# A bidirectional hybrid layer on one Trainium2 core: gate row, decays, weight rounding, key loads and z gates at other places of the order

## The chip, the core and the metric

The kernel runs on one core of one Trainium2 chip. The metric is the device time of one execution in microseconds (us). The kernel before took 1383.26 us, the median of three runs (1382.79 to 1388.96).

TensorE multiplies matrices into result tiles in PSUM, VectorE and ScalarE work on them, GpSimd does what is left of elementwise work, and SyncE issues most DMA transfers. ScalarE and GpSimd issue some as well. Each engine takes its instructions in its own order.

## The reference, cut to what matters

One layer on 2048 tokens of 1024 numbers, all in float32:

```
shift, scale, gate = split(silu(c) @ w_ada + b_ada)
h    = rmsnorm(x, norm_w) * (1 + scale) + shift
proj = h @ w_in + b_in    # na_q na_k na_v na_z (512 each), ml_q ml_k ml_v ml_o ml_z (512 each), 4 gate rows of 4
na   = neighbourhood_attention(na_q, na_k, na_v, rpb) * silu(na_z)     # 8 heads, windows of 8 x 16
q, k = split(silu(short_conv(concat(ml_q, ml_k))))
hm   = (mlstm(q, k, ml_v, gates) + flip(mlstm(flipped ...))) * sigmoid(ml_o)   # 4 heads
ml   = headnorm(hm) * ml_norm_w * silu(ml_z)
x    = x + gate * (concat(na, ml) @ w_out);  out = rmsnorm(x, final_norm_w)
```

The mLSTM runs in chunks. Inside a chunk the scores q k are multiplied by exp(Dlog - m), a triangular matrix of decays for each direction.

## The kernel before

**Matmuls.** Each float32 operand is split into a rounded part (hi) and a rest (lo), and each product is three matmuls. ScalarE rounds the weights (whi, L195), GpSimd subtracts (wlo, L196), both from the tile raw that `load_w` loads on SyncE (L193).

**Stages.** `start` normalises the tokens, multiplies them by the modulation of c and makes the first products. `tok_blocks` (L557) then goes through four blocks of 256 columns, 16 tiles of 128 tokens each, in groups of four: blocks 2 and 3 by `vo_group` (values and output gates of the mLSTM, pvo, evicted to stvo by VectorE, L499) and blocks 4 and 5 by `nav_group` (values of the attention, pv, evicted to stv, L464). Blocks 0 and 1 go by the same `vo_group` inside `start`. There are four result tiles (pp) and two stage tiles that take turns. The store of a group (d_ck L506, d_vna L468) is put off to the end of the next one. `conv_blocks` (L752) makes queries and keys of the mLSTM: pc is evicted to u by ScalarE (L773), VectorE convolves (acc_k, L808), ScalarE applies silu (L809), TensorE transposes keys (kt, L819). `phase1b` goes through four heads; in each, `ml_pass1` makes the states from tiles kv (L1013) and `ml_pass2` the outputs from tiles ck (L1058). The rest of the projections, pq (L866), fills the gaps. `phase2` is the attention and the output projection.

**The side chain.** Beside the matmuls of `tok_blocks` a chain of small jobs advances one step per token tile (`next(self.chain, None)`):
- `gate_chain` (L577) turns the gate columns into decay columns, guards and the row matrix d_mneg;
- `decays` (L685) has 16 groups. Each loads one 128x1024 tile dec (both directions) with two loads of 256 KB from d_mneg on SyncE (L702), adds the triangular mask on GpSimd (L710), raises it with eight exponentials on ScalarE (L714) and stores it to d_ck with two stores from ScalarE's queue. Two tiles take turns;
- `gate_row` (L391) makes the gate of the residual: silu(c) times the last 1024 columns of w_ada, summed by VectorE (gsum, L408 and L410) over eight loads of 512 KB into the two halves of the tile wide (L401). It advances beside the decays, one step of it per group.

The places in the order follow from the program: SyncE's loads and stores stand where the code issues them. A load whose tile is still in use holds up everything behind it.

**The passes of the mLSTM.** `close_step` (L990) runs once per chunk step. It starts a pending key load (kk, L981, 512 KB, eight in all, back from d_kna into the tiles hhi and hlo that are free by then) every second step, once they are free. `normalise` (L1131) loads the z gates of a group of four chunks (`load_z`, zt, L1070) on ScalarE's queue into a single tile; the tile is stored to d_mix from ScalarE's queue too (L1155).

## Time and profile before

| what | value |
|---|---|
| median of three runs | 1383.26 us |
| the profiled execution | 1385.16 us, span 1383.4 us |
| mean granted clock of TensorE | 0.989 |
| busy: TensorE, VectorE, ScalarE, GpSimd | 1291.3, 792.3, 531.8, 284.1 us |
| moved by DMA | 263.29 MB, mean 190 GB/s |
| blocks 2 to 5 (`tok_blocks`) | about 160 to 360 us |
| `conv_blocks` | about 360 to 554 us |
| the heads of the mLSTM | about 554 to 1010 us |

A row of a timeline gives the start, the duration, the engine, the line and the instruction with what it writes and reads, and in square brackets how long the engine had been idle before it and what ended that. PE is TensorE, DVE VectorE, ACT ScalarE, POOL GpSimd, SP SyncE; a q behind the name marks what the engine's queue issues, such as DMA transfers. A row of waits gives the waiting engine and line, the engine and line waited for, and the total, the number and the longest.

### The profile page before, as it was taken

How to read it: one execution, taken by the hardware profiler on the slowest of the kernel's cores; microseconds unless marked ns; L12 is line 12 of the kernel's file. 1: busy time of each engine (PE TensorE's matmuls, PEld its weight loads, DVE VectorE, ACT ScalarE, POOL GpSimd, SP SyncE). 2: the span in 40 equal slices, each digit the busy share in tenths (PEclk: the TensorE clock that was granted, in tenths of full speed). 3: DMA queues.
4: the chain of work that ended last, by engine and by line, in shares of the span. 5: the costliest groups of instructions: out<-in, count | busy, mean ns of one | idle time of the engine just before them, and what ended most of it. 6: DMA issues, size and time to landing. Idle time of an engine off the chain costs nothing.

```text
span 1383.4 us, 23357 instructions
## 1 busy us (share of the span) xinstructions
PE 1291.3 (93%) x8204; PEld 1104.9 (80%) x8204; DVE 792.3 (57%) x2428; ACT 531.8 (38%) x1123; POOL 284.1 (21%) x306
## 2 busy tenths in 40 slices
PE   2989998998999999999989999899998999999996
PEld 2889998998887778788878878778876777778775
DVE  6683324111355569246767866767736666667664
ACT  4642334423232233213313322323346555555552
POOL 4343212424101011001212101212201211112121
PEclk9999999999999999999999999999999999999998
DMA  9799449787557685554675788555588996867871
GB/s 321 223 290 228 122 97 238 175 204 189 149 110 210 151 191 160 164 157 144 184 219 182 229 237 284 165 159 159 176 249 251 209 228 171 187 184 183 205 182 47
DMA packets 243272, 263.29 MB, mean 190 GB/s; under 512 B 31814, under 2 KB 200006, under 8 KB 243154
## 3 DMA queue, kind: packets, MB, share of 16 engines
q1 hardware_dynamic: 151774, 186.18, 49.8%
q0 software_dynamic: 20496, 36.21, 10.8%
q10 hardware_dynamic: 70884, 39.40, 9.9%
q8 instruction: 65, 1.06, 0.3%
q14 instruction: 53, 0.43, 0.1%
HBM read 177.18 MB, written 92.72 MB: 195 GB/s over the span
## 4 chain that ended last, share of the span: by engine, by line
PE 46%; DMA 11%; issue 4%; DVE 4%; POOL 1%; ACT 1%; ACTq 0%; SPq 0%; DVEq 0%; POOLq 0%
PE pq L866 19%; PE y L1429 9%; DMA tab<-d_t 4%; PE pT L1369 3%; PE pO L1384 2%; PE pS L1341 2%; PE pi L1090 2%; DMA kv<-d_ck 2%; PE px L1088 2%; PE pc L429 2%; PE pc L430 2%; PE pc L431 2%; DMA d_mix<-zt 2%; PE dc L1036 1%; DMA d_qna<-qst 1%
## 5 line engine op out<-in xcount | busy, mean ns | idle before, releaser
L866 PE MATMUL pq<-hhi,whi_a 128*128 128x512 f32 x512 | 208.6, 407 | 1.2 <-ACT u L773 0.8
L866 PE MATMUL pq<-hlo,whi_a 128*128 128x512 f32 x512 | 208.9, 408 | 0.0
L866 PE MATMUL pq<-hhi,wlo_a 128*128 128x512 f32 x512 | 208.2, 407 | 0.0
L866 PEld LDWEIGHTS pq<-hhi,whi_a 128*128 128x128 f32 x512 | 97.3, 190 | 18.9 <-ACT u L773 1.2
L866 PEld LDWEIGHTS pq<-hlo,whi_a 128*128 128x128 f32 x512 | 97.2, 190 | 16.8 <-issue 0.5
L866 PEld LDWEIGHTS pq<-hhi,wlo_a 128*128 128x128 f32 x512 | 97.3, 190 | 16.6
L1371 ACT ACTIVATE pt<-pT 96x384 f32<-96x384 f32 (+3 forms) x128 | 65.8, 514 | 84.5 <-PE pT L1369 81.3
L1350 ACT ACTIVATE pbuf<-pbuf,mn 128x480 f32<-128x480 f32 (+5 forms) x128 | 76.1, 595 | 54.1 <-DVE mn L1349 53.8
L1429 PE MATMUL y<-hhi,whi_a 128*128 128x512 f32 x256 | 90.6, 415 | 0.5 <-ACT whi_a L1399 0.5
L1429 PE MATMUL y<-hhi,wlo_a 128*128 128x512 f32 (+1 forms) x272 | 90.6, 399 | 0.2 <-ACT y L1436 0.2
L1349 DVE CUSTOM_DVE_ANT_0 pbuf<-pS,tab 128x480 f32<-128x480 f32 (+5 forms) x128 | 63.3, 540 | 40.3 <-PE pS L1341 29.6
L840 POOL TENSOR_TENSOR wlo_a<-rawq,whi_a 128x1024 fp32r<-128x1024 f32 x20 | 48.6, 2430 | 169.8 <-ACT whi_a L839 144.9
L1112 POOL TENSOR_TENSOR hm<-hm,ck 128x128 f32<-128x128 f32 x64 | 26.4, 413 | 260.3 <-DVE hm L1111 183.4
L429 PE MATMUL pvo<-whi_b,hhi 128*128 128x256 f32 x256 | 74.1, 289 | 5.7 <-DVE stvo L499 5.7
L1093 ACT ACTIVATE num<-px,gtile 128x129 f32<-128x129 f32 x120 | 38.3, 366 | 105.7 <-PE px L1088 88.0
L1020 DVE TENSOR_SCALAR wv<-kv,gtile 128x129 f32<-128x129 f32 x120 | 38.4, 329 | 67.1 <-DMA kv<-d_ck 33.5
L1369 PE MATMUL pT<-ident,pbuf 128*128 128x128 f32 (+2 forms) x416 | 66.8, 273 | 10.0 <-DVE pbuf L1361 8.5
L1369 PEld LDWEIGHTS pT<-ident,pbuf 128*128 128x128 f32 (+2 forms) x416 | 50.3, 136 | 31.9 <-issue 11.6
L430 PE MATMUL pvo<-wlo_b,hhi 128*128 128x256 f32 x256 | 72.8, 285 | 0.0
L431 PE MATMUL pvo<-whi_b,hlo 128*128 128x256 f32 x256 | 72.8, 284 | 0.0
L714 ACT ACTIVATE dec<-dec,gtile 128x128 f32<-128x128 f32 x128 | 42.0, 392 | 71.4 <-POOL dec L710 68.3
L499 DVE TENSOR_TENSOR stvo<-pvo,brow 128x256 f32<-128x256 f32 x64 | 26.5, 419 | 68.6 <-PE pvo L431 56.4
(295 smaller groups left out, 3432.6 us busy)
## 6 DMA issues: line engine op xcount, KB each, us to landing
ck<-d_ck SPq DMA_DIRECT2D x64, 384.5 KB
kv<-d_ck SPq DMA_DIRECT2D x120, 128.5 KB
rawq<-in_w_main_dram SPq DMA_DIRECT2D x28, 512.0 KB
raw<-in_w_main_dram SPq DMA_DIRECT2D x20, 512.0 KB
d_ck<-stvo SPq DMA_DIRECT2D x16, 514.0 KB
x<-in_x_dram SPq DMA_DIRECT2D x16, 512.0 KB
wada<-in_w_ada_dram SPq DMA_DIRECT2D x32, 256.0 KB
dec<-d_mneg SPq DMA_DIRECT2D x32, 256.0 KB
```

The lines of the kernel that those rows point to most:

```text
L429: nc.tensor.matmul(ps, lhi(k), rhi(k), start=(k == 0), stop=False)
L430: nc.tensor.matmul(ps, lhi(k), rlo(k), start=False, stop=False)
L431: nc.tensor.matmul(ps, llo(k), rhi(k), start=False, stop=(k == KT - 1))
L714: nc.scalar.activation(t[:, d, o, :], t[:, d, o, :], AF.Exp, bias=self.cols["g"][:, d, h, c : c + 1])
L840: nc.gpsimd.tensor_tensor(lo[:, :, cs], raw, hi[:, :, cs].bitcast(F32), ALU.subtract)
L866: nc.tensor.matmul(patch_ps(ps) if patch else ps, w, self.htok(h, g, k, patch), start=(k == 0 and n == 0), stop=(k == KT - 1 and n == 2))
L1020: nc.vector.tensor_scalar(wv, tiles[d, i][:, 128:257], self.cols["w"][:, d, h, c : c + 1], None, ALU.mult)
L1349: nc.vector.tensor_tensor_reduce(pt[:, :nk], ps, tabs[place[u]][j][:, :nk], 1.0, 3e38, ALU.add, ALU.min, mn)
L1350: nc.scalar.activation(pt[:, :nk], pt[:, :nk], AF.Exp, bias=mn, scale=-1.0, accum_out=sums[:, j : j + 1])
L1369: nc.tensor.transpose(ps[:cs, i, :], U[u][j][:, i * cs : (i + 1) * cs], self.ident)
L1371: nc.scalar.activation(t[:cs, :nch, :], ps[:cs, :nch, :], AF.Copy)
L1429: nc.tensor.matmul(y, m[:, k, :], w[k][:, cs], start=(k == 4 and n == 0), stop=(k == 3 and n == 2))
```

## The change

- **Gate row first.** `gate_row` stands at the head of the chain, ahead of `gate_chain`. Its first step runs before block 2's loop. It loads half tiles of 256 KB (128x512), sixteen in all, three parts ahead: even parts into the tile wide, odd parts into tiles of the decays' pool. It sums into two half tiles.
- **Decays as half tiles.** One direction of a group is a tile of 128x512 (32 of them) in six buffers. In one step of the chain tile n is loaded, tile n - 2 masked, tile n - 3 raised and stored. Each load is held by an order edge behind the last matmul so far (`self.mark`); the edge orders instructions in the schedule and adds no wait at run time.
- **Weights rounded behind their load.** `raw_w` issues the load at the start of a block and gives back the rounding. It is called one half at a time: in `tok_blocks` after groups 0 and 1, in `conv_blocks` after the third and fourth tile.
- **Key loads.** Every fourth step of `close_step`, each with an order edge behind the last matmul.
- **z gates.** `load_z` issues on SyncE.

The core of the diff:

```diff
@@ load_w
-        for half in halves:
+        for part in self.raw_w(blk, slot, halves):
+            part()
+
+    def raw_w(self, blk, slot, halves=(0, 1)):
+        nc = self.nc
+        hi, lo = self.wslot[slot]
+
+        def part(half):
             raw = self.raw.tile([P, 4, 256], F32, tag=f"raw{half}", name=f"raw_{blk}_{half}")
             nc.sync.dma_start(raw, self.w_main[blk, :, 4 * half : 4 * half + 4, :])
             ks = slice(4 * half, 4 * half + 4)
-            nc.scalar.activation(hi[:, ks, :256], raw, AF.Copy)
-            nc.gpsimd.tensor_tensor(lo[:, ks, :256], raw, hi[:, ks, :256].bitcast(F32), ALU.subtract)
+
+            def run(eng=nc.gpsimd):
+                nc.scalar.activation(hi[:, ks, :256], raw, AF.Copy)
+                eng.tensor_tensor(lo[:, ks, :256], raw, hi[:, ks, :256].bitcast(F32), ALU.subtract)
+
+            return run
+
+        return [part(half) for half in halves]
@@ gate_row
-        acc = pool.tile([P, D], F32, name="gsum")
+        acc = [self.dec_tile(pool, f"gsum_{j}") for j in range(2)]
...
+            if kt % 2:
+                ts = [self.dec_tile(pool, f"ga_{kt}_{j}") for j in range(2)]
+            else:
+                ts = [buf[kt // 2 % 2][:, j * GT : (j + 1) * GT] for j in range(2)]
+            for j, t in enumerate(ts):
+                nc.sync.dma_start(t, self.w_ada[kt * P : (kt + 1) * P, 2 * D + j * GT : 2 * D + (j + 1) * GT])
...
+            for j, t in enumerate(parts.pop(kt)):
...
+                    nc.vector.scalar_tensor_tensor(a, t, cact[:, kt : kt + 1], a, ALU.mult, ALU.add)
+            if kt + 3 < KT:
+                load(kt + 3)
             yield
...
+    def dec_tile(self, pool, name):
+        return pool.tile([P, GT], F32, tag="decs", bufs=6, name=name)
@@ tok_blocks
-        self.chain = itertools.chain(self.gate_chain(chain_pool, self.gates), self.decays(chain_pool, self.gate_row(chain_pool)))
+        self.chain = itertools.chain(self.gate_row(chain_pool), self.gate_chain(chain_pool, self.gates), self.decays(chain_pool))
...
+        next(self.chain)
...
-            self.load_w(blk + 1, (blk + 1) % 2)
+            parts = self.raw_w(blk + 1, (blk + 1) % 2)
...
+                if g < 2:
+                    parts[g]()
@@ decays
+            h, gi, d = groups[n]
+            t = tiles[n] = self.dec_tile(pool, f"dec_{n}")
+            r = d * 64 + h * NC + 4 * gi
+            src = self.d_mneg[r : r + 4].rearrange("r t -> (r t)").unsqueeze(0)
+            self.behind(nc.sync.dma_start(t, src.broadcast_to([P, 512])), self.mark)
...
+        for n in range(len(groups) + 3):
+            for step, fn in ((3, raised), (2, masked), (0, load)):
+                if 0 <= n - step < len(groups):
+                    fn(n - step)
             yield
@@ conv_blocks
-                self.load_w(order[i + 1][0], (blk + 1) % 2)
+                parts = self.raw_w(order[i + 1][0], (blk + 1) % 2)
...
+                    if 2 <= 4 * sub + g < 2 + len(parts):
+                        parts[4 * sub + g - 2]()
@@ kk_jobs, behind, close_step, load_z
-            self.nc.sync.dma_start(self.kk[ct][:, e * T + T // 2 : (e + 1) * T].bitcast(F32), src)
+            self.behind(self.nc.sync.dma_start(self.kk[ct][:, e * T + T // 2 : (e + 1) * T].bitcast(F32), src), self.mark)
...
+    def behind(self, step, other):
+        order = mybir.DependencyInfo(mybir.DependencyClass.NoSync, mybir.DependencyReason.DATA)
+        self.tc.add_manual_dep(step.ins, other.ins.name, order, reason="order alone")
...
-        self.job(self.steps % 2)
+        self.job(self.steps % 4 == 0)
...
-            nc.scalar.dma_start(t, self.d_zml[4 * gi : 4 * gi + 4, :, h].rearrange("a p q -> p a q"))
+            nc.sync.dma_start(t, self.d_zml[4 * gi : 4 * gi + 4, :, h].rearrange("a p q -> p a q"))
```

The order of the engines' instructions shows what moves. VectorE, before, in block 3: the sums (gsum) stand between the evictions (stvo_3_0 to stvo_3_2 are groups of block 3, pvo_3_4 is its fifth tile).

```order
L499 TENSOR_TENSOR stvo_3_0_2193<-pvo_3_2_2264,brow1_134 128x2x128
L499 TENSOR_TENSOR stvo_3_0_2193<-pvo_3_3_2301,brow1_134 128x2x128
L410 SCALAR_TENSOR_TENSOR gsum_2330<-wide_1665,cact2_2327,gsum_2330 128x1024 x2
L499 TENSOR_TENSOR stvo_3_1_2335<-pvo_3_4_2337,brow1_134 128x2x128
L499 TENSOR_TENSOR stvo_3_1_2335<-pvo_3_5_2366,brow1_134 128x2x128
L410 SCALAR_TENSOR_TENSOR gsum_2330<-wide_1665,cact2_2327,gsum_2330 128x1024
L499 TENSOR_TENSOR stvo_3_1_2335<-pvo_3_6_2403,brow1_134 128x2x128
L410 SCALAR_TENSOR_TENSOR gsum_2330<-wide_1665,cact2_2327,gsum_2330 128x1024
L499 TENSOR_TENSOR stvo_3_1_2335<-pvo_3_7_2431,brow1_134 128x2x128
L499 TENSOR_TENSOR stvo_3_2_2462<-pvo_3_8_2464,brow1_134 128x2x128
```

After the change, the first sums stand at the end of blocks 0 and 1, between the evictions of their last groups (stvo_0_3 and stvo_1_3); the gates are 16 more columns of block 0.

```order
L431 SCALAR_TENSOR_TENSOR gsum_0_1669<-wide_1665,cact2_1666,gsum_0_1669 128x512
L524 TENSOR_TENSOR stvo_0_3_1428<-pvo_0_15_1511,brow0_133 128x2x128
L526 TENSOR_TENSOR gates_137<-pvo_0_15_1511,bgate_135 128x16
L431 SCALAR_TENSOR_TENSOR gsum_1_1670<-wide_1665,cact2_1666,gsum_1_1670 128x512
L431 SCALAR_TENSOR_TENSOR gsum_0_1669<-ga_5_0_1809,cact2_1666,gsum_0_1669 128x512
L431 SCALAR_TENSOR_TENSOR gsum_1_1670<-ga_5_1_1810,cact2_1666,gsum_1_1670 128x512
L431 SCALAR_TENSOR_TENSOR gsum_0_1669<-wide_1665,cact2_1666,gsum_0_1669 128x512
L524 TENSOR_TENSOR stvo_1_3_1552<-pvo_1_12_1554,brow1_134 128x2x128
L524 TENSOR_TENSOR stvo_1_3_1552<-pvo_1_13_1580,brow1_134 128x2x128
L524 TENSOR_TENSOR stvo_1_3_1552<-pvo_1_14_1606,brow1_134 128x2x128
L431 SCALAR_TENSOR_TENSOR gsum_1_1670<-wide_1665,cact2_1666,gsum_1_1670 128x512
L431 SCALAR_TENSOR_TENSOR gsum_0_1669<-ga_7_0_1876,cact2_1666,gsum_0_1669 128x512
```

Behind block 2's first tiles no sum is left. The second place is SyncE in block 5, with the stores d_vna of block 4's last group (stv_4_3) and of block 5's first two. Before:

```order
L468 DMA d_vna_60<-stv_4_3_3128 128x4x256
L193 DMA raw_7_0_3809<-in_w_main_dram 128x1024
L421 DMA d_gate_70<-wide_1665 1x1024
L702 DMA dec_3_2_3563<-d_mneg_62 128x512 x2
L702 DMA dec_3_3_3655<-d_mneg_62 128x512 x2
L468 DMA d_vna_60<-stv_5_0_3278 128x4x256
L193 DMA raw_7_1_3813<-in_w_main_dram 128x1024
L551 DMA d_t10_78<-d_e0_72 8x16x192 x2
L468 DMA d_vna_60<-stv_5_1_3412 128x4x256
```

Here "dec_3_2 x2" are the two loads of one 128x1024 tile. After:

```order
L728 DMA dec_17_3238<-d_mneg_62 128x512
L728 DMA dec_18_3272<-d_mneg_62 128x512
L493 DMA d_vna_60<-stv_4_3_3137 128x4x256
L728 DMA dec_19_3328<-d_mneg_62 128x512
L198 DMA raw_7_0_3866<-in_w_main_dram 128x1024
L198 DMA raw_7_1_3868<-in_w_main_dram 128x1024
L728 DMA dec_20_3362<-d_mneg_62 128x512
L576 DMA d_t10_78<-d_e0_72 8x16x192
L728 DMA dec_21_3396<-d_mneg_62 128x512
L728 DMA dec_22_3430<-d_mneg_62 128x512
L493 DMA d_vna_60<-stv_5_0_3295 128x4x256
L728 DMA dec_23_3468<-d_mneg_62 128x512
```

The loads come singly, and the stores stand between them. The third place is ScalarE in the second pass of head 2. Before, the load of the z gates of chunks 4 to 7 (zt_2_1) stands behind the store of the group before it (zt_2_0), and ahead of num of chunk 9:

```order
L1155 DMA d_mix_67<-zt_2_0_8430 128x4x128
L1093 ACTIVATE num_2_8_8544<-px_2_8_8539,gtile_2026 128x129 x2
L1070 DMA zt_2_1_8637<-d_zml_64 128x4x128
L900 ACTIVATE qst_15_2_8585<-pq_15_2_8487,bcol_93 128x512
L839 ACTIVATE whi_a_126<-rawq_17_8424 128x8x128
L869 DMA d_qna_65<-qst_15_2_8585 128x4x128 x2
L1093 ACTIVATE num_2_9_8615<-px_2_9_8610,gtile_2026 128x129 x2
L1137 ACTIVATE hm_2_1_8347<-hm_2_1_8347,mu_2_1_8577,rstd_2_1_8561 128x128 x4
```

After the change it is gone from ScalarE,

```order
L1185 DMA d_mix_67<-zt_2_0_8487 128x4x128
L1123 ACTIVATE num_2_8_8601<-px_2_8_8596,gtile_2412 128x129 x2
L865 ACTIVATE whi_a_126<-rawq_17_8481 128x8x128
L926 ACTIVATE qst_15_2_8642<-pq_15_2_8544,bcol_93 128x512
L895 DMA d_qna_65<-qst_15_2_8642 128x4x128
L1123 ACTIVATE num_2_9_8671<-px_2_9_8666,gtile_2412 128x129
L895 DMA d_qna_65<-qst_15_2_8642 128x4x128
```

and on SyncE the z gates (zt_2_1, zt_2_2) stand among the chunk loads (ck), with the first of the key loads (d_kna):

```order
L1088 DMA ck_2_10_8527<-d_ck_61 128x769
L1088 DMA ck_2_11_8578<-d_ck_61 128x769
L1100 DMA zt_2_1_8694<-d_zml_64 128x4x128
L1088 DMA ck_2_12_8645<-d_ck_61 128x769
L857 DMA rawq_18_8663<-in_w_main_dram 128x1024
L1007 DMA hhi3_1090<-d_kna_66 128x1024
L1088 DMA ck_2_13_8691<-d_ck_61 128x769
L1088 DMA ck_2_14_8737<-d_ck_61 128x769
L1088 DMA ck_2_15_8794<-d_ck_61 128x769
L1100 DMA zt_2_2_8903<-d_zml_64 128x4x128
```

So what stood behind the z gates were ScalarE's num, qst and whi_a; now it is the loads of chunks, weights and keys.

More of the change, by code (lines that the diff above doesn't have):

```diff
@@ L417, in gate_row @@
             ps = self.sp.tile([P, GT], F32, tag="sp", name=f"gp_{j}")
[L418 removed]
+            nc.tensor.matmul(ps[0:1, :], self.ones[:, 0:1], acc[j], start=True, stop=True)
             yield
@@ L683, in gate_chain, with decays @@
             yield
-    def decays(self, pool, beside):
+    def decays(self, pool):
         nc = self.nc
@@ L705, in decays @@
-        load(0)
-        load(1)
-        yield
-        for n, (h, gi) in enumerate(groups):
-            t = tiles.pop(n)
-            nc.gpsimd.tensor_tensor(t, t, mask.unsqueeze(2).broadcast_to([P, 2, 4, CH]), ALU.add)
-            for d in range(2):
-                for o in range(4):
-                    c = 4 * gi + o
-                    nc.scalar.activation(t[:, d, o, :], t[:, d, o, :], AF.Exp, bias=self.cols["g"][:, d, h, c : c + 1])
-                dst = self.d_ck[h, 4 * gi : 4 * gi + 4, :, 641 + d * CH : 641 + (d + 1) * CH].rearrange("c p t -> p c t")
-                nc.scalar.dma_start(dst, t[:, d])
-            yield
-            next(beside, None)
-            yield
-            if n + 2 < len(groups):
-                load(n + 2)
-            yield
@@ L723, in decays, with masked @@
-        for _ in beside:
-            pass
+            h, gi, d = groups[n]
[3 more added lines that the diff above has]
+            self.behind(nc.sync.dma_start(t, src.broadcast_to([P, 512])), self.mark)
+        def masked(n):
+            t = tiles[n].rearrange("p (c t) -> p c t", c=4)
+            nc.gpsimd.tensor_tensor(t, t, mask[:, groups[n][2]].unsqueeze(1).broadcast_to([P, 4, CH]), ALU.add)
```

45 lines of the change are left out of this document (23 added, 22 removed).

## The prediction

> **What bounds the kernel now.** I read the page first, then the waits of TensorE, then the timelines of the engines that end those waits.
>
> ```profile
> PE 1291.3 (93%) x8204; PEld 1104.9 (80%) x8204; DVE 792.3 (57%) x2428; ACT 531.8 (38%) x1123; POOL 284.1 (21%) x306
> ```
>
> TensorE is busy for 93% of the span and the change leaves its matmuls as they are. So time can only be won in the other 7%, 92 us, and in stretches where its clock is low. The waits of TensorE say who ends the idle stretches (total, times, longest). These rows are the ones near the change:
>
> ```profile
> PE pv L429 <- DVE stv L464: 6.5, 3, 4.7
> PE kt L819 <- ACT acc_k L809: 6.2, 3, 4.3
> PE pvo L429 <- DVE stvo L499: 5.7, 3, 2.4
> ```
>
> and, in the window from 860 to 875 us alone,
>
> ```profile
> PE px L1088 <- ACT num L1093: 5.1, 1, 5.1
> PE pi L1090 <- DVE num L1095: 0.8, 1, 0.8
> PE a L1075 <- DMA ck<-d_ck: 0.8, 1, 0.8
> ```
>
> The table by windows gives, after the engines' busy times, the granted clock, the DMA share and GB/s:
>
> ```profile
> 134.00:160.00 26.00, 25.75 (x212) 25.53 (x212) 8.31 (x18) 9.46 (x10) 11.11 (x10) 1.00 0.44 97
> 240.00:260.00 20.00, 17.79 (x139) 17.59 (x139) 4.56 (x7) 8.65 (x16) 2.53 (x3) 0.93 0.70 165
> 245.00:355.00 110.00, 101.29 (x822) 98.48 (x821) 17.35 (x39) 41.71 (x106) 38.15 (x17) 0.98 0.78 197
> 340.00:360.00 20.00, 15.34 (x111) 14.88 (x110) 3.18 (x9) 7.24 (x18) 6.35 (x3) 0.91 0.78 218
> 860.00:880.00 20.00, 13.27 (x62) 10.49 (x61) 10.71 (x35) 5.74 (x13) 3.20 (x4) 0.83 0.69 226
> ```
>
> The clock is low just where TensorE had waited. The lost clock is worth (1 - 0.93) x 20 = 1.4 us, (1 - 0.91) x 20 = 1.8 us and (1 - 0.83) x 20 = 3.4 us in the second, fourth and last of these windows, beside the waits themselves. This is an estimate, since the clock is a mean over the window.
>
> **Step 1: the gate row leaves blocks 2 and 3.** VectorE's timeline (start, duration, instruction, idle before):
>
> ```profile
> 230.99 1.29 DVE L410 SCALAR_TENSOR_TENSOR gsum<-wide,cact,gsum 128x1024 f32<-128x1024 f32 x1 [10.34 <-DMA wide<-in_w_ada_dram]
> ...
> 247.93 2.38 DVE L410 SCALAR_TENSOR_TENSOR gsum<-wide,cact,gsum 128x1024 f32<-128x1024 f32 x1 [7.95 <-DMA wide<-in_w_ada_dram]
> 250.24 1.07 DVE L499 TENSOR_TENSOR stvo<-pvo,brow 128x256 f32<-128x256 f32 x3
> ```
>
> VectorE takes its instructions in order, so the evictions of the matmul results stand behind a sum whose weights are late. Three evictions run at once after 250.24; TensorE had run out of its four result tiles. With the sums gone from there, the 5.7 us go, and with them the 1.4 us of clock: **-7.1 us**.
>
> On the clock, TensorE's row with its idle time says this:
>
> ```profile
> 238.18 0.39 PE L429 MATMUL pvo<-whi_b,hhi 128*128 128x256 f32 x1 [2.40 <-DVE stvo L499]
> ```
>
> A wait of 2.40 us stands ahead of a window with 0.93 of the clock. [...]
>
> The sums do not vanish. Sixteen half sums now stand among the evictions at 134 to 160 us, behind sixteen loads of 256 KB, 4.2 MB. VectorE is busy there for 8.31 of 26 us, and sixteen half sums add 19 us of work by half of the 2.38 us row and 10 us by half of the 1.29 us row: 27 or 19 of 26 us. I take a value near the shorter, since at 134 to 160 us VectorE is the less loaded. What decides is the DMA. It moved 97 GB/s at a share of 0.44 there, so 220 GB/s at a full one, and the 245 to 355 window gives 197/0.78 = 253. Loads of this kind by themselves ran faster at the start of the kernel (the first 20 us):
>
> ```profile
> DMA packets 3302, 6.38 MB, mean 319 GB/s; under 512 B 742, under 2 KB 870, under 8 KB 3302
> ```
>
> The 2.5 MB of now (97 GB/s x 26 us) and 4.2 MB are 6.7 MB: 21 us at 319, 30 us at 220. The four result tiles cover some 8 us (three tiles of 2.9 us, worked out in step 2). Cost: 0 to 6 us, and I take **+1**.
>
> **Step 2: decays as half tiles, one a step.** SyncE issues, in order, the decays' loads and the stores of the finished value groups:
>
> ```profile
> 322.12 0.46 SPq L468 DMA_DIRECT2D d_vna<-stv  x1
> ...
> 333.61 5.67 SPq L702 DMA_DIRECT2D dec<-d_mneg  x4
> 339.38 0.38 SPq L468 DMA_DIRECT2D d_vna<-stv  x1
> ```
>
> Two stage tiles take turns, so VectorE can't begin a group before the store of the group before last has landed:
>
> ```profile
> 305.00 0.42 DVE L464 TENSOR_TENSOR stv<-pv,brow 128x256 f32<-128x256 f32 x1 [2.36 <-PE pv L431]
> ...
> 328.76 1.42 DVE L464 TENSOR_TENSOR stv<-pv,brow 128x256 f32<-128x256 f32 x4 [10.81 <-DMA d_vna<-stv]
> 345.07 1.42 DVE L464 TENSOR_TENSOR stv<-pv,brow 128x256 f32<-128x256 f32 x4 [14.89 <-DMA d_vna<-stv]
> ```
>
> The first row ends the last group of block 4, at 305.42. Its store was issued at 322.12, 16.7 us later, and landed 6.6 us after that, when the additions at 328.76 could go on. These 23.3 us left TensorE waiting for 0.4 us of the 6.5: they are four tiles of the group between and four result tiles, so eight tiles of 2.9 us. The next store, of 339.38, landed 5.7 us later, and there TensorE had waited 4.7 us. By the program a store stands at the end of the next group, 4 x 2.9 = 11.6 us after its own; with some 6 us to land, SyncE may be 23.3 - 11.6 - 6 = 5.7 us behind for nothing. In the new order each store stands behind the load of about the step in which the next group ends, and not behind four loads that wait for a tile. The 6.5 us and 1.8 us of clock go: **-8.3 us**.
>
> What holds SyncE next is a load that waits for one of the six tiles, which is free when the store issued three steps (3 x 2.9 = 8.7 us) before has landed. That holds as long as the DMA keeps up. The same 245 to 355 us held these transfers:
>
> ```profile
> d_ck<-dec ACTq DMA_DIRECT2D x25, 256.0 KB
> dec<-d_mneg SPq DMA_DIRECT2D x22, 256.0 KB
> ```
>
> 47 x 0.262 = 12.3 MB of 197 x 110 = 21.7 MB. All 64 transfers now fall in steps 29 to 63 of the 64, about these 110 us: 16.8 + 9.4 = 26.2 MB, 238 GB/s, which at 253 GB/s is a share of 0.94. It fits, with little to spare. For waits that stay I put **+2** (0 to 6).
>
> **Step 3: weights rounded two groups after their load.** In the key convolution ScalarE stood still for weights:
>
> ```profile
> 421.66 1.06 ACT L195 ACTIVATE whi_a<-raw 128x1024 fp32r<-128x1024 f32 x1 [2.13 <-DMA raw<-in_w_main_dram]
> 422.63 0.68 ACT L773 ACTIVATE u<-pc,bcol 128x512 f32<-128x512 f32 x1
> 424.14 1.06 ACT L195 ACTIVATE whi_a<-raw 128x1024 fp32r<-128x1024 f32 x1 [0.84 <-DMA raw<-in_w_main_dram]
> ```
>
> The loads keep their place on SyncE, so the weights come no sooner, and in this block both roundings now stand ahead of the same u eviction. It then starts after 424.14 + 1.06 = 425.2 instead of 422.63, 2.6 us later, and one of the three waits of the kt row hangs on what ScalarE does behind it. Against it, acc_k_1_0 stands earlier than before, and the 4.3 us wait in block 8 should lose the 0.7 us of an eviction that now precedes the rounding. From -1 to +4; I take **+1**.
>
> **Step 4: z gates on SyncE, key loads spread.** ScalarE's queue, in the last head but one:
>
> ```profile
> 854.43 0.37 ACTq L1155 DMA_DIRECT2D d_mix<-zt  x1
> ...
> 866.34 0.37 ACTq L1070 DMA_DIRECT2D zt<-d_zml  x1
> 866.81 0.69 ACT L900 ACTIVATE qst<-pq,bcol 128x512 fp32r<-128x512 f32 x1 [10.72 <-DMA hhi<-d_kna]
> ```
>
> The load of the z gates writes the tile that the store reads, and the store needed 11.9 us, since the key loads were issued among the chunk loads at that time (the answer on DMA from 833 to 870 us):
>
> ```profile
> hhi<-d_kna SPq DMA_DIRECT2D x4, 512.0 KB
> ```
>
> These are four of the eight. Everything of ScalarE stood behind the z gates, and the px matmuls waited 5.1 us for num. Now the wait is on SyncE, and the key loads come one every fourth step and not every second. The 5.1, 0.8 and 0.8 us and 3.4 us of clock go: **-10.1 us**. What is queued behind the z gate on SyncE is chunk and weight loads. A normal wait is this:
>
> ```profile
> 897.93 0.40 ACTq L1155 DMA_DIRECT2D d_mix<-zt  x1
> ...
> 902.92 0.40 ACTq L1070 DMA_DIRECT2D zt<-d_zml  x1
> ```
>
> 5.0 us from store to load. SyncE at that time:
>
> ```profile
> 902.97 12.34 SPq L1013 DMA_DIRECT2D kv<-d_ck  x12
> ```
>
> Twelve kv loads in 12.3 us are two a step of 2.06 us, loaded three steps ahead: 6.2 us of cover for a 5.0 us wait and the load's own time. It is about used up, and four key loads now fall into this head's first pass. Cost 0 to 5; I take **+2**. The 2.06 us a step is from one head.
>
> [...]
>
> **The sum**, against the profiled execution's own 1385.2 us (span 1383.4): -7.1 + 1 - 8.3 + 2 + 1 - 10.1 + 2 = -19.5, so 1365.7. The profiled execution is 1.9 us above the median of the runs, 1383.3; the same sum against that gives **1364**.
>
> **The rivals.**
> - The DMA is full in the decays' stretch (share 0.94 by my sum, from a mean that mixes shapes). SyncE then stands at decay loads and the eight value stores are late again. At 8 us behind instead of 5.7 each costs 2 us or more: 16 us, and with step 2 most of step 1 is given back: 1383.3 - 19.5 + 16 - 2 = 1378. For it speaks the thin margin, against it that the loads are spread evenly. Chance 0.18.
> - The change does not do what it says for the z gates: the DMA stays as crowded, the wait moves to SyncE and chunk loads are late in place of num. Step 4 gives 0: 1383.3 - 19.5 + 8.1 = 1372. Against it: the eight key loads no longer stand together. Chance 0.16. [...]
> - Slower: SyncE stops at each of the sixteen z gates and the kv and chunk loads behind it come late. A kv tile is weighted by VectorE one step after its load, 2.06 us. If that is all the cover against 5.0 us, it is 16 x 2.9 = 47 us: 1383.3 - 21.5 + 47 = 1409. It decides from a wait 21.5/16 = 1.3 us beyond the cover on. Against it: TensorE is two more steps behind VectorE, which makes the 6.2 us above. Chance 0.10.
> - Better than the sum: the waits that I added are hidden, 1383.3 - 19.5 - 6 = 1358. Chance 0.06.
>
> **How the numbers follow.** The forecast, 1360 to 1370, has 0.50. The range takes in the better case, the second rival and half of the first: 1357 to 1379, 0.81. A change under 0.5% (6.9 us, so 1376.3 to 1390.2) can't be told from none. Faster: the forecast, the better case, the second rival and half of the first, 0.81. Same: the other half of the first, 0.09. Slower: 0.10.
>
> **What would show it.** Right: no pvo or pv wait for stvo or stv over 1 us; d_vna stores issued under 16 us after the last stv addition of their group; full clock from 240 to 360; no px wait for num; ScalarE without a z gate in its queue. Wrong: stvo evictions in threes with idle time for DMA ga or wide at 136 to 160; SyncE in stretches at L728 (the decay loads' new line) with pv waiting; wv waiting for kv loads after each z gate; a kt wait of over 4 us at about 420.

## The result, and the profile after

The changed kernel took 1366.62 us (median of six runs, 1360.06 to 1369.77) beside 1383.03 us for the kernel before (median of six, 1381.01 to 1388.96). The ratio is 0.9867, with a 95% interval of 0.9834 to 0.9901: 14 to 23 us less. The forecast was 1364 us, 1357 to 1379.

The profiled execution after has a span of 1358.3 us and is one of the two fastest; before it was 1383.4. Its busy times, and its waits of TensorE near the change:

```profile
PE 1284.1 (95%) x8204; PEld 1099.9 (81%) x8204; DVE 796.4 (59%) x2436; ACT 517.8 (38%) x1113; POOL 288.7 (21%) x322
```

```profile
PE pvo L454 <- DVE stvo L524: 3.2, 2, 1.9
PE pc L454 <- DVE stv L489: 3.1, 1, 3.1
PE kt L845 <- ACT acc_k L835: 2.5, 3, 1.6
```

The waits for stvo, stv and acc_k are all still there, with 8.8 us in place of 18.4. Of the px wait of 5.1 us, two short ones of 0.8 us together are left. The same windows as in the prediction:

```profile
134.00:160.00 26.00, 24.47 (x200) 24.11 (x199) 15.62 (x25) 6.60 (x7) 5.97 (x5) 1.00 0.71 234
240.00:260.00 20.00, 20.00 (x171) 20.00 (x171) 3.35 (x11) 5.85 (x9) 6.04 (x4) 1.00 0.51 127
245.00:355.00 110.00, 106.94 (x875) 105.52 (x874) 14.74 (x37) 47.16 (x131) 50.35 (x36) 1.00 0.91 220
```

The clock is full where it was 0.93 and 0.98. The gate row has put the load of the DMA into 134 to 160 us (0.44 to 0.71), and the decays theirs into 245 to 355 us (0.78 to 0.91).

To see which stage gave how much I take the first matmul of each (the row of one tile: count, shortest, median and longest in ns, first and last start in us). Before:

```profile
L429 PE MATMUL pv<-whi_a,hhi x128: 278/280/394, 256.5 to 304.4; 128*128 128x256 f32 x128
L429 PE MATMUL pc<-hhi,whi_a x128: 388/397/776, 358.4 to 508.2; 128*128 128x512 f32 x128
L866 PE MATMUL pq<-hhi,whi_a x512: 387/396/669, 554.4 to 1051.8; 128*128 128x512 f32 x171
L1341 PE MATMUL pS<-hhi,qs x192: 277/325/486, 1015.2 to 1345.7; 64*128 64x360 f32 x48, 64*128 64x480 f32 x48, 64*128 64x288 f32 x24, 64*128 64x264 f32 x24
```

After:

```profile
L454 PE MATMUL pv<-whi_a,hhi x128: 277/280/283, 254.0 to 299.1; 128*128 128x256 f32 x128
L454 PE MATMUL pc<-hhi,whi_a x128: 388/394/481, 348.2 to 492.3; 128*128 128x512 f32 x128
L892 PE MATMUL pq<-hhi,whi_a x512: 387/395/502, 538.6 to 1029.3; 128*128 128x512 f32 x171
L1371 PE MATMUL pS<-hhi,qs x192: 277/325/487, 992.8 to 1320.5; 64*128 64x360 f32 x48, 64*128 64x480 f32 x48, 64*128 64x288 f32 x24, 64*128 64x264 f32 x24
```

Differences of such starts, in us, for each profiled execution (the experiments are told below):

| kernel | to block 4 | blocks 4 and 5 | convolution | heads | rest | median of runs |
|---|---|---|---|---|---|---|
| before | 256.5 | 101.9 | 196.0 | 460.8 | 368.2 | 1383.0 |
| changed | 254.0 | 94.2 | 190.4 | 454.2 | 365.5 | 1366.6 |
| e1 changed, again | 254.7 | 94.3 | 191.7 | 454.2 | 370.2 | 1363.5 |
| e2 rounding at the load | 254.6 | 95.5 | 194.1 | 452.6 | 366.8 | 1365.2 |
| e3 z gates and keys back | 253.2 | 93.3 | 191.8 | 460.4 | 367.3 | 1367.2 |
| e4 gate row second | 249.3 | 91.0 | 197.2 | 453.7 | 371.6 | 1362.6 |
| e5 z gates back | 255.0 | 92.8 | 189.7 | 452.9 | 367.7 | 1363.7 |
| e6 keys back | 253.7 | 95.0 | 193.2 | 452.3 | 366.2 | 1364.9 |
| e7 gate row second, half the decay loads | 250.5 | 91.0 | 188.7 | 457.3 | 368.0 | 1356.9 |
| e8 gate row last | 245.8 | 107.8 | 195.3 | 453.6 | 364.9 | 1367.3 |
| e9 rneg on GpSimd | 251.3 | 96.1 | 193.1 | 456.1 | 367.2 | 1363.8 |
| e10 gate row beside the chain | 258.7 | 92.0 | 191.2 | 455.3 | 371.4 | 1364.2 |
| e11 the same, rneg on GpSimd | 260.7 | 91.1 | 191.5 | 454.7 | 368.8 | 1364.5 |
| e12 the same, loads held | 250.2 | 96.8 | 191.9 | 454.7 | 368.4 | 1359.6 |

The change leaves the last column of stages ("rest") alone, and it still goes from 364.9 to 371.6 us. So a profile tells a stage to a few us, and the 25 us between the two first profiles hold some luck. The median of e12 is that of five runs, since a sixth took 2123.12 us at a granted clock of 0.563, a slow run that its ratio leaves out too.

### The profile page after: what moved, and what is told of

It reads as the page before. It is cut to its first block, busy times and chain, and to the rows that moved or that the text cites. A ratio compares the mean times of both kernels' runs of the same rounds, so it can differ in the third digit from the quotient of the medians.

```text
span 1358.3 us, 23412 instructions
## 1 busy us (share of the span) xinstructions
PE 1284.1 (95%) x8204; PEld 1099.9 (81%) x8204; DVE 796.4 (59%) x2436; ACT 517.8 (38%) x1113; POOL 288.7 (21%) x322
## 4 chain that ended last, share of the span: by engine, by line
PE 39%; DMA 10%; DVE 7%; issue 6%; POOL 1%; SPq 1%; ACT 1%; ACTq 0%; POOLq 0%; DVEq 0%
PE pq L892 16%; PE y L1459 10%; DMA tab<-d_t 4%; DMA kv<-d_ck 3%; PE pT L1399 3%; PE pO L1414 2%; PE pS L1371 2%; DVE acc_q L834 2%; PE pi L1120 2%; PE px L1118 2%; PE dc L1066 1%; DMA hlo<-d_wo 1%; SPq L576 1%; PE a L1105 1%; DMA d_ck<-acc_k 1%
## 5 line engine op out<-in xcount | busy, mean ns | idle before, releaser
L892 PEld LDWEIGHTS pq<-hhi,whi_a 128*128 128x128 f32 x512 | 96.8, 189 | 18.0 <-ACT u L797 1.2
L892 PEld LDWEIGHTS pq<-hhi,wlo_a 128*128 128x128 f32 x512 | 96.8, 189 | 16.5
L1380 ACT ACTIVATE pbuf<-pbuf,mn 128x480 f32<-128x480 f32 (+5 forms) x128 | 76.1, 596 | 52.3 <-DVE mn L1379 52.2
```

What stands on the lines that cost most here:

```text
L892: self.mark = nc.tensor.matmul(patch_ps(ps) if patch else ps, w, self.htok(h, g, k, patch), start=(k == 0 and n == 0), stop=(k == KT - 1 a ...
L1380: nc.scalar.activation(pt[:, :nk], pt[:, :nk], AF.Exp, bias=mn, scale=-1.0, accum_out=sums[:, j : j + 1])
```

## The experiments

Ratios to the kernel before have intervals of about 0.003 either way, some 4 us. So two kernels whose intervals overlap are not told apart by their times; there the stage and the rows speak. The experiments ran in four rounds (e1 to e4, e5 to e8, e9 to e11, e12) on two chips, so between rounds the ratios compare and not the medians.

**e1, the changed kernel again**, with no edit.

> The changed kernel once more, unchanged, to see how far its own times spread. If the six times of before (1360 to 1370 us) are the spread of one kernel, the median is 1363 to 1369 us and the times again cover some 8 us; if they were a chance of one chip, they lie within 3 us, as those of the kernel before do.

1363.52 us (1360.51 to 1366.85), ratio 0.9872 (0.9843 to 0.9901). The spread is the kernel's own, and the kernel before had it too in later runs (1375.91 to 1387.62). Part of the difference between the two profiled executions (1360.06 and 1366.85 us) is the clock (mean 0.995 and 0.991), but the clock does not order all runs: of the changed kernel's six, the one of 1360.12 us had a mean clock of 0.989 and the one of 1369.77 us 0.992. Here are the windows from 340 to 360 us of the changed kernel and, below, of e1:

```profile
340.00:360.00 20.00, 16.95 (x95) 14.58 (x94) 1.42 (x4) 7.80 (x24) 7.66 (x6) 1.00 1.04 264
```

```profile
340.00:360.00 20.00, 16.85 (x85) 14.43 (x85) 1.42 (x4) 8.09 (x25) 7.57 (x6) 0.83 1.03 252
```

Nearly the same wait stands in both (3.06 us in the first and 3.15 in e1, busy 16.9 of 20); one has the full clock behind it and one 0.83.

**e2, step 3 undone.**

```diff
-            parts = self.raw_w(blk + 1, (blk + 1) % 2)
+            self.load_w(blk + 1, (blk + 1) % 2)
...
-                if g < 2:
-                    parts[g]()
...
-                parts = self.raw_w(order[i + 1][0], (blk + 1) % 2)
+                self.load_w(order[i + 1][0], (blk + 1) % 2)
```

> The changed kernel with step 3 undone: weights are rounded at the place of their load again, in tok_blocks and in conv_blocks. By my prediction, step 3 costs 1 us, so this takes about 1 us less than the changed kernel (1365 to 1366 us) and the waits of kt stay under 3 us. By the rival from the profile after, the convolution blocks gained 5.6 us through the later rounding: then this takes 4 to 6 us more (about 1371 us) and kt waits again for 5 to 6 us in total. If neither, the 5.6 us are chance of the two profiles and the time stays within 1.5 us.

1365.21 us, ratio 0.9881 (0.9853 to 0.9909). The 1.7 us to the median of e1 are inside the intervals. The convolution took 194.1 us; most kernels with the later rounding took 188.7 to 193.2, but e4 took 197.2 and e8 195.3, so the stage does not decide it either.

The rows show how little the edit moved. In block 7 ScalarE has both roundings in a row ahead of u in e2 as well (409.54, 410.95 and 411.92 us), as in the changed kernel. In block 8 an eviction u stands ahead of acc_k again, as before the change, and kt waited there for 3.65 us: it was 4.30 before, 1.59 in the changed kernel and 1.59 to 3.75 in all kernels that round later. Neither expectation is met: step 3 shows no cost, and a gain is not shown beyond that one eviction.

**e3, step 4 undone.**

```diff
-        self.job(self.steps % 4 == 0)
+        self.job(self.steps % 2)
...
-            nc.sync.dma_start(t, self.d_zml[4 * gi : 4 * gi + 4, :, h].rearrange("a p q -> p a q"))
+            nc.scalar.dma_start(t, self.d_zml[4 * gi : 4 * gi + 4, :, h].rearrange("a p q -> p a q"))
```

> The changed kernel with step 4 undone: z gates on ScalarE's queue again and a key load every second step. By my theory the 5 us wait of px for num comes back with a stretch of low clock behind it: 8 us more, about 1374 us. By the rival that the wait has only moved to SyncE (the dc waits for wv rose from 4.1 to 8.1 us), the px wait comes back but those of dc fall, and the time stays within 3 us of the changed kernel.

1367.24 us, ratio 0.9899 (0.9868 to 0.9930). The heads took 460.4 us, 6.2 more than in e1. But px did not wait for num. VectorE's timeline in the first pass of the last head, and TensorE's:

```profile
883.45 0.61 DVE L1181 SCALAR_TENSOR_TENSOR zt<-ht,mlw,zt 128x128 f32<-128x128 f32 x2 [5.85 <-DMA zt<-d_zml]
```

```profile
885.08 1.25 PE L1066 MATMUL dc<-wv,kv 128*128 128x129 f32 x4 [3.56 <-DVE wv L1050]
...
900.91 0.49 PE L1066 MATMUL dc<-wv,kv 128*128 128x129 f32 x2 [3.27 <-DVE wv L1050]
```

Ahead of the first wait the late z gates held VectorE in its order, the weights wv stood behind, and dc waited. ScalarE's queue shows why they were late:

```profile
870.05 0.37 ACTq L1185 DMA_DIRECT2D d_mix<-zt  x1
...
875.77 0.40 ACTq L1100 DMA_DIRECT2D zt<-d_zml  x1
```

5.7 us to the load, behind its store, and 7.7 us more until VectorE had it at 883.45, with two key loads issued in between. The second wait of dc came by ScalarE. Its next load of z gates stood 6.5 us behind its store, ScalarE's half of hhi stood behind that, and VectorE's half and then wv behind both (ScalarE's queue, then VectorE):

```profile
890.20 0.40 ACTq L1185 DMA_DIRECT2D d_mix<-zt  x1
896.72 0.42 ACTq L1100 DMA_DIRECT2D zt<-d_zml  x1
```

```profile
898.91 0.75 DVE L910 SCALAR_TENSOR_TENSOR hhi<-pq,bcol,hhi 128x512 fp32r<-128x512 f32 x1 [2.47 <-ACT hhi L909]
```

It is the mechanism of the prediction at another place, and who is caught behind it differs from one kernel to the next.

**e5 and e6, each half of step 4 undone alone**: the second edit of e3 without the first, and the first without the second.

> The changed kernel with the z gates on ScalarE's queue again; key loads stay at every fourth step. The heads of the mLSTM took 454.2 us in both profiles of the changed kernel and 460.4 us with z gates and keys both back. By the theory that the queue of the z gates is what counts, the heads take 459 to 461 us again and a px wait for num or a dc wait of over 3 us comes back. By the rival that the crowded key loads made the store late, so that the place of the z gates is worth nothing without them, the heads stay at 453 to 456 us and ScalarE's z gates follow their store by 5 us at most.

> The changed kernel with a key load every second step again; z gates stay on SyncE. By the theory of the queue, the heads stay at 453 to 456 us, since nothing on ScalarE waits for the store. By the rival of the crowded key loads they take 458 to 461 us, the wait now being SyncE's at a z gate, with kv or ck loads late behind it.

1363.66 us (ratio 0.9883, 0.9856 to 0.9910) and 1364.86 us (0.9901, 0.9868 to 0.9935). The heads took 452.9 and 452.3 us: in both, nothing is lost. In e5 the z gates follow their store by 5.0 us at most, where it was 6.5 in e3 and 11.9 before, and the longest wait of dc for wv is 1.7 us in e5 and 2.2 in e6, where it was 3.6 in e3. So neither theory alone is right. The 6 us are seen only with both, crowded keys and z gates on ScalarE (460.8 us before, 460.4 in e3; 452.3 to 457.3 in all other kernels), and either edit removes them. This rests on the stage and the rows of one profile each (two of the changed kernel); the intervals of the times overlap.

**e4, the gate row behind the gate chain.**

```diff
-itertools.chain(self.gate_row(chain_pool), self.gate_chain(chain_pool, self.gates), self.decays(chain_pool))
+itertools.chain(self.gate_chain(chain_pool, self.gates), self.gate_row(chain_pool), self.decays(chain_pool))
```

> The changed kernel with the gate row behind the gate chain and ahead of the decays, everything else as changed; the decays keep their steps. By my theory the sums then stand among the evictions of block 3 again, but their loads have nothing of the decays ahead of them on SyncE: waits of pvo for stvo of 2 to 5 us in total, at 205 to 245 us, in place of the 3.2 us at 155 to 167 us, so the time is within 2 us of the changed kernel. By the rival that the early place itself is worth the 7 us of step 1, it takes 5 to 7 us more, about 1373 us.

1362.58 us, ratio 0.9867 (0.9838 to 0.9895). It got to block 4 in 249.3 us, 5 us sooner than the changed kernel, with no wait at stvo. So the sums need not come first, as long as they come ahead of the decays; e8 is the other case. Blocks 4 and 5 took 91.0 us, without a wait. Then it gave all back at the first kt (TensorE's waits), since the first u of the convolution (ScalarE's timeline) came nearly as late as before (364.17 us):

```profile
PE kt L845 <- issue: 5.7, 1, 5.7
```

```profile
356.57 0.37 ACTq L741 DMA_DIRECT2D d_ck<-dec  x1
...
362.23 1.27 ACT L797 ACTIVATE u<-pc,bcol 128x512 f32<-128x512 f32 x2 [3.23 <-DMA d_t<-d_e]
```

The store of the last decay was issued at 356.57 us, in the changed kernel at 359.64, and the first u started some 5 us behind that in both (362.23 and 364.22). The profile puts u's wait down to d_t, which runs at the same time; in e9 it names the store (u at 362.67 us, after 3.39 us of waiting for d_ck from dec). By the program the tiles of u come from a pool that is opened after the pool of the decays is closed, on the same side of the memory. Before the change the last store was issued at 349.30 us, and u waited for its own matmul.

**e7, e4 with half of the decays' loads left out.** The second direction's values come from the first direction's tile.

```diff
             t = tiles[n] = self.dec_tile(pool, f"dec_{n}")
+            if d:
+                return
...
-            t = tiles[n].rearrange("p (c t) -> p c t", c=4)
+            src = tiles[n - groups[n][2]].rearrange("p (c t) -> p c t", c=4)
```

> The kernel of e4 (gate row second) that leaves out half of the decays' loads: the second direction takes its values from the tile of the first one, so the decays of the backward direction are not what the reference needs; instructions of the engines and stores stay as they were. 4.2 of 16.8 MB are gone. In e4, blocks 2 to 5 ended 8 us earlier than in the changed kernel, and 5.7 us and a stretch of low clock were lost at the first kt, since the first u waited until the last decays were stored. By the theory that the DMA is full and sets the end of the decays, they end some 15 us sooner, the kt wait goes and the time is 1353 to 1357 us. By the rival that ScalarE's exponentials or the side chain's own steps set it, the kt wait stays over 3 us and the time stays at 1361 to 1364 us.

1356.91 us, ratio 0.9836 (0.9810 to 0.9862). By the ratios that is some 4 us below e4, and the intervals overlap, so here too the rows must show it. ScalarE:

```profile
339.55 0.37 ACTq L744 DMA_DIRECT2D d_ck<-dec  x1
347.23 0.69 ACT L800 ACTIVATE u<-pc,bcol 128x512 f32<-128x512 f32 x1 [4.53 <-PE pc L456]
```

The store of the last decay is issued 17 us sooner, u waits for its own matmul again and not for a transfer, the kt wait of 5.7 us is gone, and the convolution takes 188.7 us and not 197.2. Engine work and stores were as in e4, so the decays' loads set the end of the decays, and in e4 the end of the decays held up the convolution. The edit takes away both bytes and loads that stand on SyncE, so it does not tell which of the two counts.

**e8, the gate row last.** The same line as in e4, with the order gate chain, decays, gate row.

> The changed kernel with the chain in the order gate chain, decays, gate row. The decays then start at about 205 us, where the DMA has a share of 0.34 to 0.48, in place of 245 us, where it has 0.91. By the theory that the DMA in the decays' stretch is the limit, SyncE no longer falls 17 us behind, the last decays are stored by about 335 us, the first kt does not wait, and the time is 1353 to 1357 us. By the rival that the sums bring back what step 1 removed, loads of w_ada stand behind decay loads on SyncE, VectorE stands at gsum with the stv evictions behind it, and pv waits for 4 us or more: 1362 to 1370 us.

1367.29 us, ratio 0.9919 (0.9894 to 0.9944). Block 4 began at 245.8 us, and then VectorE stood at a sum again (its timeline, and TensorE's waits from 280 to 330 us):

```profile
312.53 1.86 DVE L429 TENSOR_SCALAR gsum<-wide,cact 128x512 f32<-128x512 f32 x1 [12.77 <-DMA d_ck<-dec]
```

```profile
PE pv L454 <- DVE stv L489: 11.6, 2, 9.4
```

This is the trouble of the kernel before in another block: sums behind a crowded SyncE, evictions behind the sums. The last decay's store was issued at 316.85 us, sooner even than hoped for, and it did not help. The rival holds.

**e9, the scaling of rneg on GpSimd.**

```diff
-        nc.vector.tensor_scalar(r, r, -1.0, None, ALU.mult)
+        nc.gpsimd.tensor_scalar(r, r, -1.0, None, ALU.mult)
```

> The changed kernel with one instruction moved: the small scaling of rneg at the end of block 0 runs on GpSimd and not on VectorE. In the changed kernel SyncE stood from 140.4 to 148.3 us at the store of rneg, since VectorE did the scaling behind gsum sums that waited for loads, and the later loads of w_ada stood behind that store. By this theory SyncE no longer stands there, the two pvo waits at 154 and 164 us (3.2 us together) and the stretch of low clock behind them go, and block 4 begins at 250 to 251 us in place of 254 to 255. What that is worth at the end: by the theory that the decays' end bounds the next stages, half or less of it, 1361 to 1363 us; by the rival that each wait removed counts in full, 1358 to 1360 us.

1363.81 us, ratio 0.9886 (0.9853 to 0.9919). SyncE's timeline in the changed kernel and in e9:

```profile
140.09 0.33 SPq L418 DMA_DIRECT2D wide<-in_w_ada_dram  x1
148.30 0.35 SPq L539 DMA_DIRECT2D d_rneg<-rneg  x1
148.70 0.37 SPq L418 DMA_DIRECT2D wide<-in_w_ada_dram  x1
```

```profile
138.20 0.33 SPq L418 DMA_DIRECT2D wide<-in_w_ada_dram  x1
141.82 0.34 SPq L539 DMA_DIRECT2D d_rneg<-rneg  x1
142.26 0.92 SPq L418 DMA_DIRECT2D wide<-in_w_ada_dram  x1
```

SyncE is free again after 3.6 us and not 8.2, and block 4 begins 3 us sooner. One pvo wait of 2.8 us stayed, where both were expected to go. The first pc then waited longer for stv, 5.0 us where it was 3.1 (TensorE in e9):

```profile
347.47 0.76 PE L454 MATMUL pc<-hhi,whi_a 128*128 128x512 f32 x1 [5.01 <-DVE stv L489]
```

Blocks 4 and 5 took 96.1 us, and the time is the one of e1. Here a wait removed ahead of the decays was lost again at their end.

**e10 and e11, the gate row beside the gate chain**, so that the decays begin 13 steps sooner; the loads of the gate row go into the six half tiles alone, two parts ahead and not three; e11 with the edit of e9.

```diff
+    def side_by_side(self, one, other):
+        for _ in one:
+            next(other, None)
+            yield
+        for _ in other:
+            yield
...
-            if kt % 2:
-                ts = [self.dec_tile(pool, f"ga_{kt}_{j}") for j in range(2)]
-            else:
-                ts = [buf[kt // 2 % 2][:, j * GT : (j + 1) * GT] for j in range(2)]
+            ts = [self.dec_tile(pool, f"ga_{kt}_{j}") for j in range(2)]
```

> The changed kernel with the gate row beside the gate chain, one step of each per token tile, with loads only into the six half tiles; the decays then begin at step 17 in place of 30, about 205 us, and no sum stands among the value evictions of blocks 4 and 5. By the theory that the DMA is full in the decays' stretch and their end is what holds up SyncE and the first u, they end by about 315 us, block 6 begins at 342 to 344 us, the first kt does not wait, and the time is 1353 to 1357 us. By the rival that the sums beside the chain hold up VectorE at 136 to 190 us as before, pvo waits there for 3 us or more and the time is 1358 to 1362 us.

> The kernel of e10 with the scaling of rneg on GpSimd as in e9. By both theories together no pvo waits over 1 us are left at 136 to 190 us, and the time is 1352 to 1356 us. If e10 has no such waits, the two kernels agree within 2 us.

1364.23 us (ratio 0.9912, 0.9880 to 0.9943) and 1364.46 us (0.9900, 0.9871 to 0.9930): missed. Blocks 4 to 5 and the convolution went as hoped for (92.0 and 191.2 us; the last decay's store issued at 328 us), but block 2 did not. VectorE and TensorE in e10:

```profile
158.93 5.22 DVE L427 SCALAR_TENSOR_TENSOR gsum<-ga,cact,gsum 128x512 f32<-128x512 f32 x4 [6.99 <-DMA ga<-in_w_ada_dram]
```

```profile
165.07 0.47 PE L624 MATMUL ps_gf<-ident,wide 128*128 128x128 f32 x1 [8.51 <-DVE wide L633]
```

The loads were bound to no place, so the scheduler put the sums at 135 to 164 us again, and the gate chain's copies stood behind them. In e11 this wait was 7.6 us, so the scaling of rneg is not what made it.

**e12, e10 with the gate row four steps later and its loads held.**

```diff
-        for _ in one:
-            next(other, None)
+        for n, _ in enumerate(one):
+            if n > 3:
+                next(other, None)
             yield
...
-                nc.sync.dma_start(t, self.w_ada[kt * P : (kt + 1) * P, 2 * D + j * GT : 2 * D + (j + 1) * GT])
+                self.behind(nc.sync.dma_start(t, self.w_ada[kt * P : (kt + 1) * P, 2 * D + j * GT : 2 * D + (j + 1) * GT]), self.mark)
```

> The kernel of e10, with the gate row starting four steps later and its loads held by order edges behind the last matmul, as the decays' loads are. In e10 the scheduler pulled the sums up to 136 to 160 us, VectorE stood at a sum for 7 us, the copies for ps_gf behind it came late, and TensorE lost 8.5 us and 5 us of clock at 157 us; after that nothing waited in blocks 4 and 5 or at the first kt. With the sums held in block 2 (about 170 to 200 us), block 4 begins at 249 to 251 us as in e4, blocks 4 and 5 take 91 to 92 us and the convolution 189 to 192 us as in e10. By the theory that the place of the sums and the end of the decays are what bounds these blocks, the time is 1350 to 1355 us. By the rival that this part of the kernel gives back what it gains whatever the order, it stays at 1360 to 1364 us, with a new wait over 5 us between 160 and 370 us.

1359.63 us (1352.18 to 1363.74), ratio 0.9826 (0.9778 to 0.9873). The wait of e10 is gone and block 4 begins at 250.2 us, as expected. The time of 1350 to 1355 us did not come, nor did the 91 to 92 us for blocks 4 and 5, which took 96.8. In its profile one pv wait of 2.8 us is left at 296 us, with a clock of 0.95 and 0.88 in the two windows of 20 us from 280 us on. It is the fastest full kernel of this study, but its interval overlaps that of the changed kernel, so it is not shown to beat it.

## Why the prediction was right, point by point

The time came out 2.6 us from the forecast, but the terms did not each come out, and part of the closeness is luck: step 1 gave 3.9 us less than forecast, and the convolution 6.0 us more, for a reason that the prediction did not have. Measured is the mean of the changed kernel's two profiles against before.

| step | forecast | measured |
|---|---|---|
| 1 gate row (to block 4) | -6.1 | -2.2 |
| 2 decays (blocks 4 and 5) | -6.3 | -7.7 |
| 3 rounding (convolution) | +1 | -5.0 in the stage; step 3's part is open |
| 4 z gates and keys (heads) | -8.1 | -6.6 |
| the rest | 0 | -0.3 |
| sum | -19.5 | -21.7; by the medians -16.4 |

**Step 1: right in kind, mis-sized.** The old waits at 231 to 250 us went, as forecast. The cost of the new place was put at 1 us of 0 to 6; it was some 3 to 5, by e4, which got to block 4 five us sooner and had been 0.7 to 1.4 us ahead at 130 us already. I had counted VectorE's time and DMA's bandwidth. What I had missed is the little table step: the store of rneg stood on SyncE between the loads of w_ada and waited for a scaling that VectorE had behind its sums (8.2 us, by e9). SyncE's order shows it there; I had read that order for loads, and VectorE's only for sums and evictions. It is not the whole cost, since e9 without it still had a pvo wait of 2.8 us. Ahead of it stands, a little later than named, a sign of being wrong from the prediction: several evictions at once behind sums that had waited for wide (VectorE in the changed kernel, ahead of a pvo wait of 1.93 us; in e9 VectorE stood 6.41 us at the same sum):

```profile
161.30 1.57 DVE L431 SCALAR_TENSOR_TENSOR gsum<-wide,cact,gsum 128x512 f32<-128x512 f32 x1 [4.72 <-DMA wide<-in_w_ada_dram]
...
166.28 1.41 DVE L524 TENSOR_TENSOR stvo<-pvo,brow 128x256 f32<-128x256 f32 x4
```

**Step 2: right, with a wrong row behind it.** The stage gained 7.7 us for 6.3. The DMA share was forecast as 0.94 and came out as 0.91, but not because all of it fitted: 220 GB/s over the 110 us are 24.2 of the 26.2 MB. The rest moved later, at a share of 1.04 from 340 to 360 us, and the last decay's store went out at 359.64 us and not at 349.30 as before the change. I had a store stand at the end of the next group, which left SyncE 5.7 us. The order after has it at the end of its own group (stv_5_0 behind dec_22), which leaves 23.3 - 6 = 17 us. All of it was used. VectorE and SyncE in the changed kernel:

```profile
322.43 0.42 DVE L489 TENSOR_TENSOR stv<-pv,brow 128x256 f32<-128x256 f32 x1 [2.42 <-PE pv L456]
...
347.65 1.42 DVE L489 TENSOR_TENSOR stv<-pv,brow 128x256 f32<-128x256 f32 x4 [13.41 <-DMA d_vna<-stv]
```

```profile
340.00 0.54 SPq L493 DMA_DIRECT2D d_vna<-stv  x1
```

The group that ended at 322.85 had its store issued 17.2 us later, and TensorE waited the 3.1 us that were left over. SyncE was late since it stood at decay loads for tiles whose stores had not landed (its waits from 240 to 360 us, where the same wait was 55.7 us before):

```profile
SPq L728 <- DMA d_ck<-dec: 41.2, 14, 7.4
```

So the first rival, a full DMA, is half true. It did not bring back the old waits, but the decays now end later than before, and e4, e7 and e9 show that this end took back what was gained ahead of it. Whether bytes or SyncE's order set it is not shown.

**Step 3: wrong in sign, by its premise that the weights come no sooner.** I let both roundings delay the same u by 2.6 us and took +1. ScalarE in the changed kernel:

```profile
407.15 1.06 ACT L202 ACTIVATE whi_a<-raw 128x1024 fp32r<-128x1024 f32 x1 [2.75 <-DMA raw<-in_w_main_dram]
408.40 1.06 ACT L202 ACTIVATE whi_a<-raw 128x1024 fp32r<-128x1024 f32 x1 [0.20 <-DMA raw<-in_w_main_dram]
409.37 0.67 ACT L797 ACTIVATE u<-pc,bcol 128x512 f32<-128x512 f32 x1
```

The two roundings stand in a row, as read from the order, and u followed 2.2 us behind the start of the first, where it had been 1.0. But the weights came sooner. SyncE issued their loads before the change at

```profile
414.61 0.90 SPq L193 DMA_DIRECT2D raw<-in_w_main_dram  x2
```

which is 56.2 us behind the first pc (358.4), and after it at 400.82 us, 52.6 behind the first pc (348.2). So u started 61.2 us behind the first pc, where it had been 64.2 and the forecast comes to 66.8, and a kt wait of 1.72 us at 430.62 us was gone. That goes with the loads and not with the place of the rounding: it is gone in e2 too, whose loads were issued 52.3 us behind its first pc, and it stands with 1.82 us in e8, which rounds late but issued its loads at 56.2. Why the loads were issued sooner was not tested.

The wait in block 8 came down from 4.3 to 1.6 us, where the prediction credited 0.7. Between the kernels that round late it varies from 1.59 to 3.75 us, so how much of the 5.0 us is the place of the rounding and how much faster loads stays open.

**Step 4: right, and the reason was only half of it.** The 6.6 us are near the 8.1. I had the z gates' queue and the spread of the keys as two parts of one gain; e5 and e6 show that either gives the whole. The prediction also read the crowd too small: beside the four key loads into hhi, the same answer on DMA has three into hlo, so seven of the eight.

```profile
hlo<-d_kna SPq DMA_DIRECT2D x3, 512.0 KB
```

The 2 us that I charged for z gates on SyncE can't be seen in the stage: with them there (e6) the heads take 452.3 us, with them on ScalarE (e5) 452.9. But part of the wait has moved. SyncE stood at z gates for 35.1 us in the changed kernel, and TensorE's waits for weighted kv tiles rose from 4.1 us to 8.1, and to 9.6 in e1 (SyncE after; TensorE before and after):

```profile
SPq L1100 <- DMA d_mix<-zt: 35.1, 13, 4.6
```

```profile
PE dc L1036 <- DVE wv L1020: 4.1, 4, 1.3
```

```profile
PE dc L1066 <- DVE wv L1050: 8.1, 7, 2.3
```

They are 6.6 us in e5, so the z gates' place can explain only a part of the rise. With the keys spread, the issuer of the z gates made a difference of 1 us in the heads (e5 against e1); with the keys crowded it made 8 us (e3 against e6).

**The rivals and the signs.** Slower by waits at sixteen z gates did not come: SyncE stood at 13 of them for the store, but for 4.6 us at most, under the 6.2 us of cover. The better case, 1358 us, is what the first profile alone would have shown; the median is not there. Of the signs of being right, two failed: stvo was still waited for by up to 1.9 us, and a d_vna store was issued 17.2 us after its group. The full clock from 240 us on came in the first profile and not in e1 (0.97 from 245 to 355 us).

## What to carry to other kernels

Before crediting a removed wait in full, look for the next thing that ends at a fixed time whatever the engines do: here the last decay's store, set by transfers (issued at 356.57 us in e4, and at 339.55 in e7 without half of the decays' loads), which took back what e4 and e9 gained ahead of it. When a step moves, write down every instruction of every engine that will now stand between its loads on the issuing queue, also the small ones of other jobs. And where two edits are made against one wait, undo each alone and both together: either may be enough. Look then at the order of the instructions as well: undoing step 3 in the program (e2) left ScalarE's order in block 7 as it was.

## What the runs showed of the hardware that I had not expected

- A wait of TensorE of 3.06 us was followed by a full clock (1.00) in one execution, and one of 3.15 us at the same place by 0.83 of it over 20 us in another of the same kernel (windows of e1, above). Before the change a wait of 2.40 us, with one of 1.09 us 5.5 us ahead of it, stood ahead of 0.93. So in these traces the length of a wait alone did not tell whether the clock drops, and the clock terms of the prediction (1.4, 1.8 and 3.4 us) hold for the execution that they were read from.
- Twelve later runs of the kernel before reached from 1372.47 to 1385.52 us, while its first three lay from 1382.79 to 1388.96. Three runs are too few for a difference of 5 us here.
